# Operands of two projections split by prompt and sample columns, in a decoder layer with experts on one core

## The chip, the cores and the metric

The kernel runs on one core of a Trainium2 chip. The metric is the time of one execution on the device in microseconds (us). The engines are named as the profile does: PE (TensorE, matmul), PEld (its weight loads), DVE (VectorE), ACT (ScalarE), POOL (GpSimd) and SP (SyncE, which here only issues DMAs). A "q" behind a name (ACTq, SPq) marks what the engine's sequencer does, mostly the issue of a DMA.

## What is computed

One layer for a prompt of 512 tokens and a sample group of 8 sequences of 4 tokens (32 columns), which share all weights. Cut to what matters here:

```
z  = x @ w_in + b_in                    # split among the parts below
ya = head_norm(mlstm(...)) * sigmoid(og)        # branch A, 1024 wide
yb = sliding_window_attention(...)              # branch B, 1024 wide
mix = (sigmoid(ga) * (ya @ w_a) + sigmoid(gb) * (yb @ w_b)) @ w_out
x = LN1(ALPHA * x + mix)
x = LN2(ALPHA * x + hierarchical_moe(x))        # 32 experts
x = LN3(ALPHA * x + sigmoid(x @ w_pg) * (p @ w_pp))
```

Outputs are the new x and the new states, among them `k_s` and `v_s`: per sample sequence the last 128 rows of keys and values, of which 124 are copied from the old buffers and four are new. `p` are the embedding rows of the layer (512 + 32 rows of 256).

## The kernel before

All activations of the dense stages lie transposed: partitions are features, columns are the 544 tokens (512 of the prompt, then 32 of the samples: `NG = SEQ + NS`). A float32 operand is taken apart into a high and a low part of type fp32r (`split_from`: ACT casts the high part, L569; DVE subtracts it, L570), and a product is three matmuls (`three`, L656 to L658: high x high, high x low, low x high).

**Jobs.** A job is a block of 256 weight columns. `stream` runs the jobs in a fixed sequence: w_in's parts, among them the branch gates (GA writes `sigA`, GB writes `sigB`, four jobs each), then w_a (four jobs), w_b (four) and w_out (four). A job has two units of 128 columns. `fetch` loads the job's 1 MB of weights on SP's queue into one of two `raw` buffers, `prepare` splits a unit's weights into `wH` and `wL` (two buffers each) one unit ahead. A unit of w_a or w_b has two halves: columns 0 to 255 and 256 to 543, so that only the second half contains samples. For each of the eight 128-row blocks of the operand (k = 0 to 7) a half does three matmuls into a PSUM buffer `pj`, of which there are two. `mix_a` (L908) multiplies w_a's result with `sigA`, `mix_b` (L916, and L917 on POOL) multiplies w_b's result with `sigB`, adds, and splits the sum into `mix`, w_out's operand.

**What runs beside them.** `weave(upto, (generator, rate), ...)` runs the jobs up to a count and gives each generator so many of its steps per half unit. During GA and GB these are `swa` (the prompt's attention, with exponentials on ACT; its results go into `qsT`, which becomes `yb`) and `sample_mlstm` (it writes the sample columns of `ya` at its end). During w_a it is `sample_swa`, the samples' attention, which writes the sample columns of `qsT` (= `yb`) at its end (L1550). During w_b it is `embeddings`, which transposes the embedding rows and stores them.

**What sets the order.** The calls above give each instruction a priority. Before the kernel is built, a scheduler replays the instructions with estimated times and puts each engine's into one fixed list: an instruction goes as soon as its inputs, its buffer and its engine are free in that replay, so one of low priority can move far ahead of where it is written. On the chip each engine follows its list in order, and whatever waits there holds all that is behind it. `tc.issue_after(x)` puts DMAs behind x on their engine. A tile that takes over memory of an earlier one waits for the last user of that tile, DMAs that read it included. Pools open and close like stacks, from a left and a right end of the memory.

**The transitions that the change touches.** After GB, the sigmoids of `sigA` and `sigB` are one ACT instruction each (L1417). `split_tiles` splits `ya` into eight pieces of 544 columns (`yaH`, `yaL`). Once `ya` is split, its memory becomes `r_p`, and ACT's queue loads 2 MB of x into it (L1433). In `sample_swa`, `k_new` (the new keys, transposed back by PE and copied by ACT, L1466) and `v_new` are stored into the outputs by 16 DMAs on ACT's queue (L1557), and two DMAs on POOL copy the 124 old rows (L1555). The samples' keys come in four loads (`kb`, POOL, L1458), are transposed by PE (L1478) and copied by ACT into `KT` (L1479); L1492 are the scores, L1539 and L1546 the transposes and products of the values. After w_a, `split_tiles` splits `yb` (`ybH`, `ybL`), and the first step of `embeddings` loads the rows (`pin`, five DMAs on ACT's queue, L1575); PE transposes them (L1581), ACT copies them into `pT_in` (L1582), and a DMA stores that for later.

After w_out come the first LayerNorm and the routing, then the experts, whose weights (6 MB each) stream in through SP's queue, the first of them already during w_out, and then the tail.

Of the kernel before, what the change touches and what calls it, by code (L numbers as in the profile page):

```python
# [9 lines left out]
F32 = mybir.dt.float32  # L10
F32R = mybir.dt.float32r
# [3 lines left out]
AF = mybir.ActivationFunctionType  # L15
# [4 lines left out]
P = 128  # L20
D = 1024
KD = D // P
SEQ = 512
NT = SEQ // P
SB, ST = 8, 4
NS = SB * ST
# [4 lines left out]
WIN = 128  # L31
# [5 lines left out]
DPLE = 256  # L37
# [487 lines left out]
def tile_decoder_step(ctx: ExitStack, tc: tile.TileContext, *aps):  # L525
    nc = tc.nc
    A = dict(zip(_INS + _CONSTS + _OUT_NAMES, aps))
    sy, act, dve, pe, gp = nc.sync, nc.scalar, nc.vector, nc.tensor, nc.gpsimd

    def pool(name, bufs=1, side="left", space=None, stack=ctx):  # L530
        if space is None:
            return stack.enter_context(tc.tile_pool(name=name, bufs=bufs, side=side, reuse_waits="tile"))
        return stack.enter_context(tc.tile_pool(name=name, bufs=bufs, space=space))
# [16 lines left out]
    left = ctx.enter_context(ExitStack())  # L550
# [6 lines left out]
    right = ctx.enter_context(ExitStack())  # L557
# [7 lines left out]
    def pst(shape, tag):  # L565
        return ps.tile(shape, F32, name=tag, tag=tag)

    def split_from(H, L, src, eng=dve):
        act.copy(out=H, in_=src)  # L569
        return eng.tensor_tensor(out=L, in0=src, in1=H.bitcast(F32), op=ALU.subtract)  # L570
# [7 lines left out]
    NG = SEQ + NS  # L578
# [42 lines left out]
    for pp in range(2):  # L621
        gp.dma_start(
            out=brow[16 + 4 * pp:20 + 4 * pp, :].rearrange("j (a d) -> j a d", a=2),
            in_=b_in[C_QS + 512 * pp:C_QS + 512 * (pp + 1)].rearrange("(a j d) -> j a d", a=2, j=4),
# [136 lines left out]
    def weave(upto, *others):  # L761

        nonlocal flow
        others = [[g, rate, 0.0, True] for g, rate in others]
        while state["done"] < upto:
            next(flow)
            for o in others:
                o[2] += o[1]
                while o[3] and o[2] >= 1.0:
                    o[2] -= 1.0  # L770
                    o[3] = next(o[0], "end") != "end"
        if state["pending"]:
            state["pending"]()
            state["pending"] = None
        live = [o for o in others if o[3]]
        while live:
            live = [o for o in live if next(o[0], "end") != "end"]
# [26 lines left out]
    ya = ZA.tile([P, KD, NG], F32, name="ya", tag="za")  # L804
# [30 lines left out]
    tiles = {}  # L835
# [66 lines left out]
    N_GA, N_GB, N_WA, N_WB, N_WO = 22, 26, 30, 34, 38  # L902
# [77 lines left out]
    for r in two:  # L980
# [9 lines left out]
                   in_=wg_in[:].rearrange("p k (a b) -> p k a b", a=2))  # L990
# [84 lines left out]
    def chain(*gens):  # L1075
        for g in gens:
            yield from g
# [335 lines left out]

    weave(N_GB, (swa(), 2.6), (sample_mlstm(pool("smp", stack=sws)), 0.8))
    early.close()
    for g in (tiles["sigA"], tiles["sigB"]):
        act.activation(out=g, in_=g, func=AF.Sigmoid)  # L1417
    yb = qsT


    Z2 = pool("split", bufs=2, side="right", stack=right)

    def split_tiles(where, src, name):
        H, L = (where.tile([P, KD, NG], F32R, name=name + x, tag="split") for x in "HL")
        for k in range(KD):
            split_from(H[:, k], L[:, k], src[:, k])
        return H, L

    tiles["ya"] = split_tiles(Z2, ya, "ya")
    r_more = ZA.tile([P, NT * D + 256], F32, name="r_p", tag="za")  # L1430
    tiles["r_p"] = r_more[:, 0:NT * D].rearrange("p (t d) -> p t d", t=NT)
    shift1 = r_more[:, NT * D:]
# [2 lines left out]
    def sample_swa(Q):  # L1435
# [28 lines left out]
        for pp in range(2):  # L1464
# [4 lines left out]
                        in_=kss[:].rearrange("p a (b t) -> p a b t", t=ST))  # L1469
        yield  # L1470
        for b0 in range(0, SB, 2):
# [4 lines left out]
            for b in range(2):  # L1476
                for pp in range(2):
                    pe.transpose(out=pt[:, b, pp], in_=kb[:, b, pp * P:(pp + 1) * P], identity=ident)  # L1478
            act.copy(out=KT[:, b0:b0 + 2, :, 0:WIN].rearrange("p b a w -> p (b a) w"),  # L1479
                     in_=pt[:].rearrange("p b a w -> p (b a) w"))  # L1480
# [44 lines left out]
        def place(g):  # L1525

            pp, par = g // 2, g % 2
            return slice(64 * par, 64 * par + 64), pp, slice(64 * par + 32 * pp, 64 * par + 32 * pp + 32)

        for g in range(SKV):  # L1530
            hp, pp, rows = place(g)
            pe.matmul(pO[pp][hp], v_new[0:NS, g * SD:(g + 1) * SD], pT4[:, :, rows], start=True, stop=False)
        for b0 in range(0, SB, 2):
# [9 lines left out]
            for b in range(2):  # L1543
                for g in range(SKV):
                    hp, pp, rows = place(g)
# [3 lines left out]
        for pp in range(2):  # L1549
            dve.tensor_copy(out=qsT[:, 4 * pp:4 * pp + 4, SEQ:].rearrange("p j (b t) -> p j b t", t=ST),  # L1550
                            in_=pO[pp][:, :, 0:16].rearrange("p b (j t) -> p j b t", t=ST)[:, :, :, ::-1])
        yield
        for o, src, new in ((ko, bk, k_new[:].rearrange("s a d -> s (a d)")), (vo, bv_, v_new)):
            with tc.issue_after(last.ins):
                gp.dma_start(out=o[:, 0:WIN - ST, :], in_=src[:, ST:WIN, :])  # L1555
            for b in range(SB):
                act.dma_start(out=o[b, WIN - ST:, :], in_=new[ST * b:ST * (b + 1)])  # L1557

    with ExitStack() as scope:
        weave(N_WA, (sample_swa(pool("smp", stack=scope)), 1.5))  # L1560
    late = right.enter_context(ExitStack())
    Z3 = pool("splitb", bufs=2, side="right", stack=late)
    tiles["yb"] = split_tiles(Z3, yb, "yb")
    tiles["mix"] = tuple(Z2.tile([P, KD, NG], F32R, name="mix" + x, tag="split") for x in "HL")

    pTd = dram.tile([P, 2, NG], F32, name="pTd")

    def embeddings(Q):
        pT = Q.tile([P, 2, NG], F32, name="pT_in", bufs=1)
        pins = []  # L1570
        for t in range(NT + 1):
            rows = P if t < NT else NS
            pins.append(Q.tile([P, DPLE], F32, name="pin", bufs=NT + 1)[:rows])
            src = A["p_prompt"][0, 0, t * P:(t + 1) * P] if t < NT else A["p_sample"][0].rearrange("b t d -> (b t) d")
            act.dma_start(out=pins[t], in_=src)  # L1575
        yield
        for t, pin in enumerate(pins):
            rows = pin.shape[0]
            tp = pst([P, 2, rows], "tp")
            for k in range(2):  # L1580
                pe.transpose(out=tp[:, k], in_=pin[:, k * P:(k + 1) * P], identity=ident[:rows, :rows])  # L1581
            act.copy(out=pT[:, :, t * P:t * P + rows], in_=tp)  # L1582
            yield
        act.dma_start(out=pTd[:], in_=pT)
        yield

    with ExitStack() as scope:
        weave(N_WB, (embeddings(pool("ples", stack=scope)), 0.5))
# [145 lines left out]
    for t, st in zip(order, stats):  # L1734
        x1 = x1s[t]
        rows = x1.shape[0]
# [35 lines left out]
    with ExitStack() as scope:  # L1772
# [28 lines left out]
        def rt(name, shape, dt=F32):  # L1801
            return R.tile(shape, dt, name=name)
# [144 lines left out]
        with tc.issue_after(tokens.ins):  # L1947
# [13 lines left out]
            which = rt("which", [P, 4])  # L1961
# [44 lines left out]
    late = [(0, [(x1s[t], x1d[t * P:(t + 1) * P], "rb") for t in range(NT)] + [(*pg_half(0), "al")])]  # L2006
# [181 lines left out]
    for k in range(KD):  # L2188
        H, L, src = pg(k, 0, 512, D), pg(k, 1, 512, D), pg_in[1][:, k]
# [51 lines left out]
```

## Time and profile before

| what | value |
|---|---|
| median of 3 runs | 1151.51 us (1149.5 to 1151.61) |
| the profiled execution, its own time | 1153.13 us |
| its span, first to last instruction | 1151.3 us |
| mean granted clock of PE | 0.966 |
| PE busy | 1046.8 us (91%) |
| DVE, ACT, POOL busy | 483.7, 334.8, 245.4 us |
| HBM traffic | 248.44 MB read, 20.13 MB written |

The dense stages with w_a, w_b and w_out lie from about 457 to 640 us of the span, the experts from about 680 to 1062, the tail behind them. In a row of a timeline stand the start, the duration, the engine, the line, the operation, the tiles written and read, the shapes and how many instructions were merged; in brackets how long the engine had been idle and what ended that. In a table by stretches, each engine's busy time is followed by its count of instructions; PEclk is the clock granted to PE, where 1.00 is the full one.

### The profile page before, as it was taken

Reading aid. Unit: us, or ns where it says so; the run is one execution under the profiler, and the core shown is the slowest. Engines: PE = TensorE matmul, PEld = TensorE weight load, DVE = VectorE, ACT = ScalarE, POOL = GpSimd, SP = SyncE. Lnnn points to the kernel's source line nnn. Section 1 sums busy time; section 2 is a strip of 40 time slices with the busy share of each in tenths; the row PEclk is TensorE's granted clock in tenths of the full one; section 3 lists DMA queues with packets and bytes.
Section 4 is the critical chain, followed back from the end, with each engine's and each line's share of the span. In section 5 each row is a group of like instructions: output and inputs, shape, how many; then the busy total and the mean of one; then the engine's idle time right before and its main releaser. Section 6 shows DMA issues by size and latency. Waiting matters only on the chain. (4 is left out here: it accounts for less than half of the span.)

```text
span 1151.3 us, 26865 instructions
## 1 busy us (share of the span) xinstructions
PE 1046.8 (91%) x10359; PEld 821.0 (71%) x10360; DVE 483.7 (42%) x1245; ACT 334.8 (29%) x682; POOL 245.4 (21%) x368
## 2 busy tenths in 40 slices
PE   7999999999999999998999788775999979877987
PEld 6988999999877779898989544432555545544765
DVE  3646533546555556264566611111112111111886
ACT  5411224223454744323311311110111111212531
POOL 5000000401346562202410111101222222221021
PEclk8999999999999999898999989989899999999998
DMA  7321322223214334543389959999999999999711
GB/s 245 75 74 38 111 73 75 79 74 109 99 38 147 108 102 136 204 125 103 113 294 374 362 196 405 422 418 422 419 420 419 418 423 418 423 418 385 285 50 60
DMA packets 99024, 263.65 MB, mean 229 GB/s; under 512 B 11326, under 2 KB 58708, under 8 KB 85092
## 3 DMA queue, kind: packets, MB, share of 16 engines
q1 hardware_dynamic: 84100, 232.96, 53.0%
q0 software_dynamic: 9440, 25.24, 6.2%
q10 hardware_dynamic: 5408, 4.39, 1.3%
q8 instruction: 53, 0.87, 0.3%
q14 instruction: 23, 0.19, 0.1%
HBM read 248.44 MB, written 20.13 MB: 233 GB/s over the span
## 5 line engine op out<-in xcount | busy, mean ns | idle before, releaser
L656 PE MATMUL pj<-xH,wH 128*128 128x256 f32 (+1 forms) x672 | 197.9, 295 | 0.0
L658 PE MATMUL pj<-xH,wL 128*128 128x256 f32 (+1 forms) x672 | 197.2, 293 | 0.0
L657 PE MATMUL pj<-xL,wH 128*128 128x256 f32 (+1 forms) x672 | 196.8, 293 | 0.0
L569 ACT CAST wH<-raw 128x1024 fp32r<-128x1024 f32 x76 | 79.6, 1048 | 244.0 <-PE pj L657 155.5
L656 PEld LDWEIGHTS pj<-xH,wH 128*128 128x128 f32 x672 | 126.8, 189 | 6.3 <-issue 4.9
L658 PEld LDWEIGHTS pj<-xH,wL 128*128 128x128 f32 x672 | 126.4, 188 | 4.7 <-issue 4.3
L657 PEld LDWEIGHTS pj<-xL,wH 128*128 128x128 f32 x672 | 126.8, 189 | 2.7 <-issue 2.2
L570 DVE TENSOR_TENSOR wL<-raw,wH 128x1024 fp32r<-128x1024 f32 x76 | 94.8, 1249 | 74.0 <-ACT wH L569 72.9
L300 PE MATMUL psG<-w,xT 128*32 128x256 f32 x1152 | 73.0, 395 | 22.4 <-issue 13.8
L428 ACT ACTIVATE sg<-psG 128x128 f32<-128x128 f32 x50 | 13.9, 277 | 267.2 <-PE psG L300 267.2
L463 DVE COPY hT<-psH 128x128 f32<-128x128 f32 x50 | 14.6, 292 | 150.7 <-PE psH L305 144.5
L300 PEld LDWEIGHTS psG<-w,xT 128*32 128x32 f32 x1152 | 37.5, 112 | 49.5 <-issue 30.2
L1275 POOL TENSOR_SCALAR lg<-lg,sm 128x256 f32<-128x256 f32 (+1 forms) x64 | 55.2, 876 | 28.4 <-DVE sm L1272 17.3
L458 DVE COPY xT<-xg 128x256 f32 (+1 forms) x50 | 14.8, 295 | 109.8 <-PE psG L300 109.5
L263 POOL DMA_INDIRECT ybuf<-ysb,idy x50 | 49.5, 990 | 45.7 <-POOL idy L260 34.2
L300 PE MATMUL psG<-gu3a,xT 128*32 128x256 f32 x576 | 36.5, 395 | 14.8 <-DMA gu3a<-in_w_eu_dram 8.7
L415 ACT ACTIVATE xg<-psX,gcol 128x128 f32 (+1 forms) x100 | 36.3, 467 | 42.8 <-PE psX L293 42.8
L470 DVE SCALAR_TENSOR_TENSOR ysb<-psY,ywt,r_p 128x256 f32<-128x256 f32 x50 | 24.2, 484 | 57.1 <-PE psY L314 57.1
L656 PE MATMUL pj<-wH,xH 128*128 128x256 f32 x160 | 47.4, 296 | 0.0
L657 PE MATMUL pj<-wL,xH 128*128 128x256 f32 x160 | 45.1, 282 | 0.0
L658 PE MATMUL pj<-wH,xL 128*128 128x256 f32 x160 | 44.9, 280 | 0.0
L300 PE MATMUL psG<-w2a,xT 128*32 128x256 f32 x448 | 28.5, 397 | 14.9 <-issue 7.8
(609 smaller groups left out, 2263.3 us busy)
## 6 DMA issues: line engine op xcount, KB each, us to landing
w<-in_w_eg_dram SPq DMA_DIRECT2D x26, 1024.0 KB
w<-in_w_eu_dram SPq DMA_DIRECT2D x26, 1024.0 KB
w<-in_w_ed_dram SPq DMA_DIRECT2D x26, 1024.0 KB
raw<-in_w_in_dram SPq DMA_DIRECT2D x22, 1024.0 KB
w2d<-in_w_ed_dram SPq DMA_DIRECT2D x14, 1024.0 KB
r_p<-in_w_ed_dram SPq DMA_DIRECT2D x14, 1024.0 KB
w2a<-in_w_eg_dram SPq DMA_DIRECT2D x7, 1024.0 KB
w2a<-in_w_eu_dram SPq DMA_DIRECT2D x7, 1024.0 KB
```

The costliest lines, as they stand in the source:

```text
L263: gp.indirect_dma_start(out=ybuf.rearrange("t (q d) -> (t q) d", q=4), out_offset=bass.IndirectOffsetOnAxis(ap=idy[:, r:r + 1], axis=0), i ...
L300: m = pe.matmul(psG[32 * q:32 * q + 32], xT[:, k], W[s][half][:, :, kh, P * q:P * q + P], start=k == 0, stop=k == KD - 1)
L415: m = act.activation(out=out, in_=psX[:, k], func=AF.Identity, bias=gcol[:, 1, k:k + 1], scale=gcol[:, 0, k:k + 1])
L458: dve.tensor_copy(out=xT[:], in_=src).then_inc(S["cx"], 1)
L463: dve.tensor_copy(out=hT[:], in_=psH[:]).then_inc(S["ch"], 1)
L470: dve.scalar_tensor_tensor(out=ysb[:, r], in0=psY[:], scalar=ywt[:, bass.ds(i1, 1)], in1=shift, op0=ALU.mult, op1=ALU.add).then_inc(S["cy" ...
L569: act.copy(out=H, in_=src)
L570: return eng.tensor_tensor(out=L, in0=src, in1=H.bitcast(F32), op=ALU.subtract)
L656: pe.matmul(out, lh(k), rh(k), start=start and i == 0, stop=False)
L657: pe.matmul(out, lh(k), rl(k), start=False, stop=False)
L658: pe.matmul(out, ll(k), rh(k), start=False, stop=stop and i == len(ks) - 1)
L1275: gp.tensor_scalar(out=lg[:, par, j, 0:nk], in0=lg[:, par, j, 0:nk], scalar1=sm[:, 2, par, j:j + 1], scalar2=None, op0=ALU.mult)
```

## The change

- The sigmoids of `sigA` and `sigB` become four instructions each, for two of the eight blocks at a time. Those of `sigA` stay ahead of w_a in the program's order, those of `sigB` are woven into w_a.
- `split_tiles` splits the prompt's 512 columns only, in eight pieces, and is a generator; `split_samples` splits the 32 sample columns of all eight blocks with one cast and one subtraction. For `ya` both follow each other ahead of w_a. For `yb` the prompt's pieces are woven into w_a, and the sample pair follows behind w_a.
- The pool of the split `yb` opens ahead of w_a, under the samples' attention, on the other end of the memory.
- The embedding rows get a pool of their own that opens ahead of w_a, and are loaded by five DMAs on SP's queue, woven into w_a ahead of the pieces of `yb`. `pT_in` stays in the pool that opens at w_b, which now begins where the samples' attention had its pool.
- The new keys and values are stored by eight DMAs on POOL's queue (one per token of the four, for all eight sequences) in place of 16 on ACT's, and they stand in the `issue_after` block of the copies of the old rows.

```diff
-    for g in (tiles["sigA"], tiles["sigB"]):
-        act.activation(out=g, in_=g, func=AF.Sigmoid)
+    def sigmoids(g):
+        for i in range(0, KD, 2):
+            act.activation(out=g[:, i:i + 2], in_=g[:, i:i + 2], func=AF.Sigmoid)
+            yield
+    for _ in sigmoids(tiles["sigA"]):
+        pass
...
-    def split_tiles(where, src, name):
-        H, L = (where.tile([P, KD, NG], F32R, name=name + x, tag="split") for x in "HL")
+    def split_tiles(which, where, src, name):
+        H, L = tiles[which] = tuple(where.tile([P, KD, NG], F32R, name=name + x, tag="split") for x in "HL")
         for k in range(KD):
-            split_from(H[:, k], L[:, k], src[:, k])
-        return H, L
-    tiles["ya"] = split_tiles(Z2, ya, "ya")
+            split_from(H[:, k, 0:SEQ], L[:, k, 0:SEQ], src[:, k, 0:SEQ])
+            yield
+    def split_samples(which, src):
+        H, L = (t[:, :, SEQ:] for t in tiles[which])
+        split_from(H, L, src[:, :, SEQ:])
+    for _ in split_tiles("ya", Z2, ya, "ya"):
+        pass
+    split_samples("ya", ya)
...
             with tc.issue_after(last.ins):
                 gp.dma_start(out=o[:, 0:WIN - ST, :], in_=src[:, ST:WIN, :])
-            for b in range(SB):
-                act.dma_start(out=o[b, WIN - ST:, :], in_=new[ST * b:ST * (b + 1)])
-    with ExitStack() as scope:
-        weave(N_WA, (sample_swa(pool("smp", stack=scope)), 1.5))
+                for t in range(ST):
+                    gp.dma_start(out=o[:, WIN - ST + t, :], in_=new[t:NS:ST])
     late = right.enter_context(ExitStack())
     Z3 = pool("splitb", bufs=2, side="right", stack=late)
-    tiles["yb"] = split_tiles(Z3, yb, "yb")
+    rows_p = left.enter_context(ExitStack())
+    pin_pool = pool("pins", stack=rows_p)
+    pins = []
+    def load_rows():
+        yield
+        for t in range(NT + 1):
...
+            sy.dma_start(out=pins[t], in_=src)
+            yield
+    with ExitStack() as scope:
+        weave(N_WA, (sample_swa(pool("smp", stack=scope)), 1.5), (sigmoids(tiles["sigB"]), 1.0),
+              (chain(load_rows(), split_tiles("yb", Z3, yb, "yb")), 0.9))
+    split_samples("yb", yb)
...
     def embeddings(Q):
         pT = Q.tile([P, 2, NG], F32, name="pT_in", bufs=1)
-        pins = []
-        for t in range(NT + 1):
...
-            act.dma_start(out=pins[t], in_=src)
-        yield
```

More of the change, by code (lines that the diff above doesn't have):

```diff
@@ L1555, in sample_swa @@
                 gp.dma_start(out=o[:, 0:WIN - ST, :], in_=src[:, ST:WIN, :])
-            for b in range(SB):
-                act.dma_start(out=o[b, WIN - ST:, :], in_=new[ST * b:ST * (b + 1)])
-    with ExitStack() as scope:
-        weave(N_WA, (sample_swa(pool("smp", stack=scope)), 1.5))
+                for t in range(ST):
+                    gp.dma_start(out=o[:, WIN - ST + t, :], in_=new[t:NS:ST])
     late = right.enter_context(ExitStack())
     Z3 = pool("splitb", bufs=2, side="right", stack=late)
-    tiles["yb"] = split_tiles(Z3, yb, "yb")
+    rows_p = left.enter_context(ExitStack())
[4 more added lines that the diff above has]
+        for t in range(NT + 1):
+            rows = P if t < NT else NS
+            pins.append(pin_pool.tile([P, DPLE], F32, name="pin", bufs=NT + 1)[:rows])
+            src = A["p_prompt"][0, 0, t * P:(t + 1) * P] if t < NT else A["p_sample"][0].rearrange("b t d -> (b t) d")
+            sy.dma_start(out=pins[t], in_=src)
[4 more added lines that the diff above has]
+    split_samples("yb", yb)
     tiles["mix"] = tuple(Z2.tile([P, KD, NG], F32R, name="mix" + x, tag="split") for x in "HL")
@@ L1569, in embeddings @@
         pT = Q.tile([P, 2, NG], F32, name="pT_in", bufs=1)
-        pins = []
-        for t in range(NT + 1):
[L1572 to L1575, printed above, removed]
-        yield
         for t, pin in enumerate(pins):
```

## The prediction

> **What bounds the kernel now.** I read the busy time by stretch first, to see where TensorE stands still, then the timelines of single engines around those places.
>
> ```profile
> core 0: us, PE busy (x) PEld busy (x) DVE busy (x) ACT busy (x) POOL busy (x), PEclk, DMA share, GB/s
> 285.00:457.00 172.00, 172.00 (x1243) 140.13 (x1243) 93.86 (x326) 88.58 (x247) 77.59 (x107) 1.00 0.33 109
> 457.00:474.00 17.00, 17.00 (x138) 16.91 (x136) 6.41 (x11) 8.18 (x7) 8.35 (x15) 1.00 0.74 255
> 474.00:484.00 10.00, 7.40 (x43) 5.39 (x42) 1.74 (x3) 3.33 (x6) 1.44 (x2) 0.66 0.47 164
> 521.00:535.00 14.00, 10.36 (x70) 9.74 (x67) 7.72 (x14) 6.09 (x12) 0.54 (x1) 0.76 0.51 116
> 664.00:684.00 20.00, 18.00 (x100) 10.94 (x104) 4.42 (x22) 4.25 (x8) 2.35 (x3) 0.82 0.31 113
> 709.00:1062.00 353.00, 291.56 (x4571) 162.94 (x4561) 58.85 (x187) 61.49 (x148) 68.54 (x114) 0.96 1.02 419
> ```
>
> From 285 to 474, TensorE (PE) is busy all the time: the dense stages are bound by it, and work of other engines beside it is free. In the w_a and w_b stages it has two holes, 474 to 484 and 521 to 535, each followed by a spell at a lower granted clock (0.66 and 0.76 on average). From 709 to 1062 DMA is full with expert weights. That stream is not tied to the clock on the wall: in 664 to 684 DMA is only 31% busy, because the prefetched buffers are full and the stream waits for the experts to start. So what the dense stages save moves the whole rest forward.
>
> **Hole A (in w_a).** Timelines of ACT and PE:
>
> ```profile
> 459.31 0.41 ACTq L1433 DMA_DIRECT2D r_p<-in_x_prompt_dram  x1
> 464.29 10.78 ACTq L1557 DMA_DIRECT2D out_dram<-k_new  x8
> 465.82 0.66 ACTq L1557 DMA_DIRECT2D out_dram<-k_new  x2
> 473.17 1.90 ACTq L1557 DMA_DIRECT2D out_dram<-k_new  x2
> 475.17 1.04 ACT L569 CAST wH<-raw 128x1024 fp32r<-128x1024 f32 x1 [9.96 <-DMA raw<-in_w_a_dram]
> 476.12 0.58 ACT L1479 COPY KT<-tp 128x512 f32<-128x512 f32 x1
> 470.32 0.60 PE L1478 MATMUL tp<-keep,kb 128*128 128x128 f32 x4
> 470.67 0.36 PE L656 MATMUL pj<-yaH,wH 128*128 128x256 f32 x1
> 470.87 0.29 PE L657 MATMUL pj<-yaL,wH 128*128 128x256 f32 x1
> 472.52 0.30 PE L656 MATMUL pj<-yaH,wH 128*128 128x288 f32 x1
> 473.86 0.29 PE L657 MATMUL pj<-yaL,wH 128*128 128x288 f32 x1
> 476.75 0.65 PE L1492 MATMUL nm<-KT,QT 64*32 64x132 f32 x4 [2.60 <-ACT KT L1479]
> 483.49 0.29 PE L658 MATMUL pj<-yaH,wL 128*128 128x288 f32 x1
> 484.30 0.43 PE L1492 MATMUL nm<-KT,QT 64*32 64x132 f32 x8
> 484.66 0.39 PE L658 MATMUL pj<-yaH,wL 128*128 128x256 f32 x1
> ```
>
> PE waits for the first KT copy, which stands on ACT behind the w_a cast, and that stands behind the eight DMA issues of k_new. An issue takes 0.3 to 0.4 us, yet the eight last 10.78 us: the sixth ends at 466.48, the last two come at 473.17 and just before 475. By the semaphores in the trace, the hardware DMAs of SP and ACT share eight completion semaphores in turn, and these two issues wait until the previous users of theirs have landed: the 2 MB load of r_p from 459.31 and a w_a fetch. So ACT stands still for transfers that nobody there needs.
>
> The size: at full rate a 288-wide matmul takes 0.134 us (473.86 - 472.52, ten steps), a 256-wide one 0.118 (472.52 - 470.87, 14 steps), four transposes 0.35 (470.67 - 470.32), eight score products 0.36 (484.66 - 484.30). From 474.00 to 483.62, PE did 16 score products (0.72), 8 transposes (0.70) and 13 wide matmuls (1.74): 3.2 us of work in 9.6. Hole A costs 6.4 us.
>
> **Hole B (start of w_b).**
>
> ```profile
> 520.64 0.66 PE L1546 MATMUL sp<-pT_s,kb 128*64 128x32 f32 x16
> 521.23 0.49 DVE L1550 COPY qsT<-sp 128x128 f32<-128x128 f32 x2
> 521.57 0.64 ACT L569 CAST ybH<-qsT 128x544 fp32r<-128x544 f32 x1
> 521.69 1.23 DVE L570 TENSOR_TENSOR wL<-raw,wH 128x1024 fp32r<-128x1024 f32 x1
> 521.76 1.80 ACTq L1575 DMA_DIRECT2D pin<-in_p_prompt_dram  x1
> 522.26 0.39 PE L656 MATMUL pj<-ybH,wH 128*128 128x256 f32 x1 [0.96 <-ACT ybH L569]
> 522.84 5.17 DVE L570 TENSOR_TENSOR ybL<-qsT,ybH 128x544 fp32r<-128x544 f32 x8
> 524.45 0.66 PE L1581 MATMUL tp<-keep,pin 128*128 128x128 f32 x2 [1.67 <-DMA pin<-in_p_prompt_dram]
> 527.48 0.66 PE L1581 MATMUL tp<-keep,pin 128*128 128x128 f32 x2 [1.00 <-DMA pin<-in_p_prompt_dram]
> 534.34 0.30 PE L658 MATMUL pj<-ybH,wL 128*128 128x288 f32 x1
> ```
>
> Each of the eight splits of yb covers all 544 columns, so none starts before the sample columns of qsT are written (521.72); then PE waits for splits and, in its own order, for the embedding rows. From 521.2 to 534.48 it did one unit of w_b, 24 x 0.118 + 24 x 0.134 = 6.05 us, and five transposes, 0.44: 6.5 us of work in 13.3. Hole B costs 6.8 us.
>
> **The change, part by part.**
>
> Stores of new keys and values: 16 ACT issues become 8 on GpSimd, behind the two 992 KB copies. With them goes ACT's standstill, so hole A goes: -6.4 us. What is late next there is the KT copy itself, right after its transposes (470.67 plus 0.58), before PE needs it at 474.00.
>
> ```profile
> 513.66 0.60 POOL L1555 DMA_DIRECT2D out_dram<-in_state_swa_k_dram  x1
> out_dram<-in_state_swa_k_dram POOLq DMA_DIRECT2D x1, 992.0 KB, 8.2
> out_dram<-in_state_swa_v_dram POOLq DMA_DIRECT2D x1, 992.0 KB, 9.5
> POOL sigA L917 <- DVE sigB L916: 19.6, 1, 19.6
> ```
>
> GpSimd pays 8 x 0.60 = 4.8 us, inside 19.6 us in which it waits for w_b's first result. Its own DMAs also wait in turn; the longest such wait is a 992 KB landing, 8.2 us. Behind the eight issues on its queue is only the first sum of w_b (L917), which nothing on PE needs at once. Without that cover the cost is 4.8 to 13 us of GpSimd time.
>
> yb: the prompt parts (8 casts of about 0.6, 8 subtractions of about 0.65 us) move into w_a, where they may run once the attention of the prompt is done; ACT was busy 8.18 of 17 us there, with the standstill counted as idle. They go one by one, so a waiting cast of weights loses at most 0.64 us. What is left at w_b's start is one pair for 256 sample columns: 521.72, plus at most 0.64 and 0.65, with the weight cast and its subtraction (1.0 and 1.2 us) perhaps ahead of them. Only the second half of the first unit needs it, 24 x 0.118 = 2.8 us after 521.2. Between 0 and 1.5 us is left of the hole by this; I take 0.5.
>
> Embedding rows: five issues move from ACT (one took 1.80 us) to SP, into w_a, and PE's two waits (1.67 and 1.00) go. On SP they stand among the w_a and w_b fetches; 0.5 MB more run beside r_p and a w_a fetch, at the 255 GB/s of that stretch 2.1 us. That fetch had landed by 475. Its cast comes due when the unit ends whose second half starts at 472.52 (at full rate 24 x 0.134 = 3.2 us later, 475.7), and the next unit covers six us more, of which cast and subtraction take 2.3: I take 0; if the fetch were 6 us later it would cost 2 to 3.
>
> A new wait: the transposed rows (pT_in) now lie where the sample attention's pool begins, over k_new, and their first copy on ACT must wait for the k_new stores. Those queue behind the 992 KB copy, which landed at 513.66 + 8.2 = 521.9, 0.7 us after w_b could begin, plus the four stores. The third transpose of rows waits for that copy's buffer on PE. Bounds: 0, and 6.8 (all of hole B back). I take 1.5, nearer to the lower end, as the landing is only 0.7 us late.
>
> ya: the pieces narrow from 544 to 512 columns and one sample pair comes on top, at most 0.64 + 0.65 us; PE has no hole at w_a's start (17.00 of 17.00 busy), so 0; uncovered, 1.3.
>
> Sigmoids: 3.84 us at once becomes four pieces of about 1 us each. The pieces can go where the scheduler finds ACT free, as the whole one did:
>
> ```profile
> L829 ACT ACTIVATE sigA<-pj,bcol x8: 480/494/495, 293.7 to 378.0; 128x288 f32<-128x288 f32 x8
> 380.57 1.28 ACT L1417 ACT_TABLE_LOAD   x1
> 381.87 3.84 ACT L1417 ACTIVATE sigA<-sigA 128x4352 f32<-128x4352 f32 x1
> 385.99 1.28 ACT L1269 ACT_TABLE_LOAD   x1
> ```
>
> It ran right after its last input (378.0), between exponentials, with a table load on each side: 6.7 us of ACT. Each of sigA's four pieces can have such a pair, and sigB's first two as well if they fall among the attention's exponentials: five more blocks of 1.28 + 1 + 1.28 = 3.6 us, 18 us on ACT, which was busy 88.58 of 172. The 6.7 us block left PE at 172.00 of 172.00, so I take 0. Bounds: 0 and 18.
>
> [...]
>
> **Sum.** -6.4 - 6.8 + 0.5 + 1.5 = -11.2 us. The profiled execution took 1153.13 us with a span of 1151.3, so it would take 1141.9; it lies 1.6 above the median of the runs, 1151.51, and against that the sum gives 1140.3. The runs lie within 2.1 us; 0.2% (2.3 us) is about what a measurement can tell from none.
>
> **Rivals.**
>
> Slower, by sigmoid pieces: if PE stood still for each of the five added blocks, because its accumulators are emptied and its weights cast by ACT, the sum is 1140.3 + 18 = 1158. It decides from 2.3 us lost per block (11.2 / 5). For it: the pieces can only go into the exponentials. Against: the full PE row around a longer block. [...]
>
> A wait takes hole B's place: pT_in behind k_new holds ACT, and with it the sample split and the casts. If the stores land 5 us after w_b's start instead of 1 to 2, it costs about 3.5 more plus the low clock after a hole (2 us): 1140.3 + 5.5 = 1146. For it: the second copy landed 9.5 us after its issue, and stores go in the same queue.
>
> Not what it says: hole A stays, because other DMAs in w_a (the rows on SP) wait in turn for the same r_p load and hold the fetches behind them: 1140.3 + 6.4 = 1147. Against: SP has six us in hand there.
>
> [...]
>
> Same: the expert stream swallows it, 1151. For it: 419 GB/s from 709 on. Against: DMA's lull before.
>
> **How the numbers follow.** Forecast 0.60 (1137.5 to 1143.5); the new wait 0.13 and hole A staying 0.09 (both to 1148); slower 0.10; same 0.05; the rest, 0.03, is faster than 1137. Faster than 0.2%: 0.60 + 0.13 + 0.09 + 0.03 = 0.85. The range from 1137 to 1148 holds 0.82.
>
> **What would show it.** Right: no row of ACT issuing k_new, no wait of PE for KT over 1 us, casts of ybH during w_a, clock 1.00 in both stages, w_b's first matmuls right after the last of w_a, the first expert transpose some 11 us earlier. Wrong: a PE gap at w_b's start ended by ACT pT_in; more than ten table loads with PE idle before 457; a w_a fetch that ends a wait of the cast.

## The result, and the profile after

The changed kernel takes 1145.1 us (median of 20 runs, 1142.19 to 1150.82) against 1150.33 us of the kernel before (20 runs, 1146.79 to 1157.08): a ratio of 0.995, 95% interval 0.9934 to 0.9965, so 4 to 7.6 us faster (5.8 by the ratio, 5.2 by the medians). The forecast was 1140.3, which was 11.2 us less than its own baseline. The profiled execution took 1144.28 us with a span of 1142.3.

Both holes are gone. The busy time by stretch of the changed kernel; the last three stretches answer to 521:535, 664:684 and 709:1062 of before, moved by what the dense stages won:

```profile
core 0: us, PE busy (x) PEld busy (x) DVE busy (x) ACT busy (x) POOL busy (x), PEclk, DMA share, GB/s
285.00:457.00 172.00, 172.00 (x1245) 140.14 (x1244) 94.74 (x330) 102.93 (x260) 78.56 (x109) 1.00 0.34 112
474.00:484.00 10.00, 10.00 (x106) 8.24 (x105) 4.06 (x7) 3.23 (x5) 2.16 (x3) 1.00 0.54 179
517.00:531.00 14.00, 14.00 (x114) 14.00 (x113) 6.71 (x12) 4.43 (x7) 4.17 (x7) 1.00 0.31 76
654.00:674.00 20.00, 17.99 (x108) 11.03 (x110) 4.42 (x22) 3.96 (x7) 2.36 (x3) 0.84 0.33 115
699.00:1052.00 353.00, 292.09 (x4554) 163.08 (x4550) 58.40 (x184) 61.01 (x148) 68.61 (x113) 0.95 1.02 419
```

PE is full and at full clock where it was 7.40 of 10 and 10.36 of 14 busy at 0.66 and 0.76. In w_a, ACT now has no DMA issue of k_new between its casts, and the prompt part of yb goes there (timeline of ACT), while GpSimd issues the stores behind the two copies (timeline of POOL):

```profile
460.40 0.35 ACT L1478 COPY k_new<-tp 32x256 f32<-32x256 f32 x1
460.65 1.11 ACT L1419 ACTIVATE sigB<-sigB 128x1088 f32<-128x1088 f32 x1
461.67 3.21 ACT L569 CAST ybH<-qsT 128x512 fp32r<-128x512 f32 x6
465.08 1.05 ACT L569 CAST wH<-raw 128x1024 fp32r<-128x1024 f32 x1 [0.21 <-PE pj L657]
466.60 0.59 ACT L1491 COPY KT<-tp 128x512 f32<-128x512 f32 x1 [0.46 <-PE tp L1490]
...
507.64 2.10 POOL L1569 DMA_DIRECT2D out_dram<-k_new  x4
516.63 1.03 POOL L1569 DMA_DIRECT2D out_dram<-v_new  x2 [3.42 <-DMA out_dram<-in_state_swa_k_dram]
521.36 0.73 POOL L917 TENSOR_TENSOR sigA<-sigA,sigB 128x256 f32<-128x256 f32 x1 [3.70 <-DVE sigB L916]
```

In this pair of profiles the whole forecast is there: the last product of w_b starts at 567.32 instead of 577.62 and the first expert's transpose at 669.17 instead of 679.57, 10.4 us earlier. Yet the medians differ by 5.2. The experiments ask where the other half is.

### The profile page after: what moved, and what is told of

Its sections match the earlier page's. It is cut to its first block, busy times and chain, and to the rows that moved or that the text cites. A ratio compares the mean times of both kernels' runs of the same rounds, so it can differ in the third digit from the quotient of the medians.

```text
span 1142.3 us, 26870 instructions
## 1 busy us (share of the span) xinstructions
PE 1043.9 (91%) x10359; PEld 819.3 (72%) x10360; DVE 484.3 (42%) x1247; ACT 346.7 (30%) x698; POOL 249.9 (22%) x376
```

## The experiments

All ratios are to the kernel before, run beside them, five rounds, with the 95% interval.

**Both kernels once more.** No edit.

> The kernel before, unchanged, for a second profile. The changed kernel's dense stages gained 12.3 us from the first matmuls after the start to the first expert transpose, but the medians of 20 runs moved only 5.2. Theory A (spread): the trace of before first shown was simply a slow execution; in a second one the holes in w_a and w_b are as long as in the first within 1 us, and the experts take some 3 us less than the 384.4 us (first transpose to last down product) of the first. Theory B (the holes vary): the holes are together several us shorter in this execution than 13.2.

> The changed kernel, unchanged, for a second profile. Theory A (spread): dense stages as in the first trace, no hole in w_a or w_b, first expert transpose at 667 to 669 us; five rounds give a ratio to before of 0.990 to 0.998. Theory C (the experts give it back): the experts take 4 to 5 us longer than in both traces of before, again and again, so that the sum of the parts is the 5 us measured.

Before: 1152.16 us, ratio 1.0012 (0.9991 to 1.0033). After: 1145.41 us, 0.9949 (0.9925 to 0.9972). The gain of 5 to 6 us is firm. But the second profile of the kernel before is another one than the first: the same holes, at two thirds of the price. Here is hole A in three stretches of 3.41 us of the busy time view (length, PE's busy time, and so on; the granted clock is third from the end), before (first three lines) and again_before:

```profile
473.04:476.45 3.41, 1.11 (x9) 0.87 (x7) 0.20 (x1) 1.28 (x2) 0.00 (x0) 1.00 0.24 87
476.45:479.86 3.41, 3.11 (x16) 1.79 (x16) 1.36 (x2) 0.83 (x2) 0.73 (x1) 0.50 0.31 105
479.86:483.28 3.42, 3.42 (x20) 2.88 (x20) 0.00 (x0) 0.90 (x2) 0.71 (x1) 0.50 0.98 345
...
475.24:478.66 3.42, 1.55 (x14) 0.97 (x15) 1.56 (x2) 2.04 (x3) 0.24 (x1) 1.00 0.01 2
478.66:482.07 3.41, 3.41 (x21) 2.69 (x20) 0.00 (x0) 0.98 (x3) 1.20 (x2) 0.50 0.96 323
482.07:485.48 3.41, 3.41 (x34) 3.07 (x33) 2.00 (x4) 1.05 (x1) 0.00 (x0) 1.00 0.37 143
```

In the 14 profiles the granted clock stood at 0.50 only in pieces of 3.41 us (or multiples), on a grid whose phase against the kernel's start differs from profile to profile (0.3 to 3.2 us). How busy PE was in a stretch went with the clock of the next one, as counted over the grid stretches that have a clock on record for themselves and for the next (4622):

```
at full clock, PE busy under 0.40 of the stretch:  next one at 0.50 in  117 of 118
               0.40 to 0.50:                                            21 of 57
               over 0.50:                                               40 of 4164
at 0.50,       PE busy under 0.75:                 next one at 0.50 in   73 of 73
               0.75 to 0.85:                                            33 of 44
               over 0.85:                                               13 of 166
```

So, by these counts, a gap of 2.3 us may or may not leave one stretch under 0.40 busy (2.05 us idle); it depends on where the grid falls. In again_before the grid cuts the gap: the stretch shown is 0.45 busy (1.55 of 3.42) and one of the 21 that a low one followed. Each piece costs a full PE 1.7 us, an estimate from its length and its clock (3.41 x 0.50).

**Half of the change at a time.** Stores alone, and yb's prompt part and rows alone (both with whole sigmoids):

```diff
 # stores_only: the kernel before with
-            for b in range(SB):
-                act.dma_start(out=o[b, WIN - ST:, :], in_=new[ST * b:ST * (b + 1)])
+                for t in range(ST):
+                    gp.dma_start(out=o[:, WIN - ST + t, :], in_=new[t:NS:ST])
 # yb_rows_only: the kernel before with split_tiles, split_samples and load_rows of the change
```

> Before, with the 16 stores of new keys and values on ACT replaced by eight on GpSimd, nothing else. My theory: hole A (474 to 484) is gone, the first expert transpose comes 6.4 us earlier than in before (679.6 less 6.4 = 673.2, start-up aside), the hole at w_b's start stays at about 6.8. Rival (issue time only): only the eight issues of 0.3 to 0.4 us are saved, the gain is under 3 us and PE still waits for KT.

> Before, with ya and yb split by prompt and sample columns, yb's prompt part and the embedding rows during w_a; the stores stay on ACT's queue and the sigmoids stay whole. My theory: the hole at w_b's start is gone (6.8 us), the hole in w_a stays or grows, since the five loads of rows take turns with the stores' DMAs; first expert transpose 5 to 7 us earlier than in before. Rival: the ACT standstill now also holds the pieces of yb, so that w_b still waits, gain under 3 us.

Stores alone: 1155.18 us, 1.0035 (1.0013 to 1.0057). Yb and rows alone: 1150.65 us, 1.0001 (0.9981 to 1.002). Neither gains what I expected; together with the rest they gain 5 to 6. PE's waits from 470 to 530 (total, number, longest), stores_only first, then yb_rows_only:

```profile
PE tp L1581 <- DMA pin<-in_p_prompt_dram: 2.9, 1, 2.9
PE pj L656 <- ACT ybH L569: 1.0, 1, 1.0
PE pj L657 <- DVE ybL L570: 0.8, 1, 0.8
...
PE nm L1499 <- ACT KT L1486: 2.3, 1, 2.3
```

Each closes its own hole. But with hole A closed, PE comes to w_b 4.5 to 5.4 us earlier (first product 516.8, against 522.3 in before and 521.3 in again_before). The idle time of hole B grows, from 3.6 and 2.3 us to 4.7: the rows' loads are issued when w_b begins, and PE's transposes of rows begin 7.6 us after the first of these issues, against 3.8 us in the kernel before (520.68 to 524.45). That the 992 KB copies beside them are the reason is my reading (timelines of POOL and ACT, stores_only; the second copy landed at 521.5, 10.6 us after its issue, and the transposes of rows began at 522.8):

```profile
510.90 0.61 POOL L1555 DMA_DIRECT2D out_dram<-in_state_swa_v_dram  x1
515.24 0.36 ACTq L1575 DMA_DIRECT2D pin<-in_p_prompt_dram  x1
516.33 0.34 ACTq L1575 DMA_DIRECT2D pin<-in_p_prompt_dram  x1
L1581 PE MATMUL tp<-keep,pin x4: 415/421/446, 522.8 to 524.8; 128*128 128x128 f32 x4
```

**Stores alone, again.** No new edit.

> The kernel before with the stores on GpSimd alone, once more, because the first time it came out 4 us slower than the kernel before while its dense stages were no longer. If that was a chance of its clock pieces (7 of 3.41 us between w_b and the experts, 5 in the comparison) and of the late last expert weights (PE waited 2.5 us), the time comes to 1149 to 1152 now. If it belongs to the kernel, it comes to 1154 to 1156 again, and the trace again shows PE waiting 2.5 us at the last expert, and a wait of over 4 us in all at the start of w_b.

1152.96 us, 1.0004 (0.998 to 1.0028). The wait for rows is there again, 3.4 us, so stores alone win nothing; that they lose 4 us was partly chance. That they lose something (1.0035 and 1.0004) stays open.

**Which half of hole B.** Stores with the rows early, and stores with the yb split, each without the other:

```diff
 # stores_rows: stores_only with load_rows in w_a, yb split whole after it
+        weave(N_WA, (sample_swa(pool("smp", stack=scope)), 1.5), (load_rows(), 0.9))
 # stores_yb: stores_only with yb's prompt part split in w_a, rows still on ACT in embeddings
+        weave(N_WA, (sample_swa(pool("smp", stack=scope)), 1.5),
+              (split_tiles("yb", Z3, yb, "yb"), 0.9))
```

> The kernel before with the stores on GpSimd and the embedding rows loaded on SP during w_a; yb is still split whole, behind the sample columns, and the sigmoids are whole. Two looks at stores alone showed hole A gone, and hole B with 4.7 and 5.2 us of PE standing still, of which the rows' landing made 2.9 and 3.4; those rows were issued 515 to 518 and landed behind the 992 KB copies. Theory 'rows took it': with the rows early that part goes; 1.0 us (ybH) and at most 1.5 us (splits) of standing still remain, at a low clock in some executions only: 1147 to 1150. Rival 'both parts are needed': PE, no longer held by rows, waits for the splits instead, which come one in 0.65 us, eight in 5.2: 1150 to 1153.

> The kernel before with the stores on GpSimd and yb's prompt part split during w_a; the rows are still loaded on ACT when w_b begins, and the sigmoids are whole. Theory 'rows took it': the waits for ybH and ybL go, and the wait for the rows remains if their products stand as early in PE's order as before (2.9 to 3.4 us and the clock behind it: 1149 to 1153); if the schedule puts them later, because nothing of w_b waits any more, there is no wait and the time is that of the changed kernel, 1145 to 1147. Rival: the splits are hole B's whole price and the rows none: 1145 to 1147 with a wait for rows still in the trace.

Stores and rows: 1146.5 us, 0.9963 (0.9945 to 0.998), PE without a gap over 0.5 us from 470 to 530: the change's gain without the yb split. Stores and yb: 1148.01 us, 0.998 (0.9961 to 1.0), one gap of 1.06 us in w_a (for a weight split on DVE) and none in w_b, because PE's order now has the rows' products later (the first at 526.6). With A closed, hole B is closed with either half, but in both runs the order changed with the edit. In stores_rows PE also does the last value products of the samples at 512.95 instead of 515.21, so that the casts of yb begin at 513.9 instead of 516.1, while PE still has products of w_a to do. What each half is worth at an unchanged order is not shown.

**The change without its stores, and without its pieces.** The two remaining parts taken back, one each:

```diff
 # act_stores_back: the changed kernel with
-                for t in range(ST):
-                    gp.dma_start(out=o[:, WIN - ST + t, :], in_=new[t:NS:ST])
+            for b in range(SB):
+                act.dma_start(out=o[b, WIN - ST:, :], in_=new[ST * b:ST * (b + 1)])
 # whole_sigmoids: the changed kernel with
+    for g in (tiles["sigA"], tiles["sigB"]):
+        act.activation(out=g, in_=g, func=AF.Sigmoid)
```

> The changed kernel with the sixteen stores of new keys and values put back on ACT. Six profiled executions so far show the granted clock at 0.50 only in pieces that are multiples of 3.41 us, and a piece follows a stretch in which PE stood still. Theory 'clock by chance': hole A comes back with 2.3 to 2.6 us of PE standing still (the wait for KT), plus no, one or two pieces of low clock at 1.7 us of lost work each, other in each execution; so the time goes from 1145.4 to between 1147.5 and 1151, and the rest of the stage stays as in the changed kernel (no wait for embedding rows, no wait for ybH). Rival 'full price': the hole costs the 6.4 us that I summed from one profile in every execution: 1151.8. Rival 'stores gain nothing': stores on GpSimd alone made the kernel before 4 us slower, so taking them off again makes the changed kernel faster or leaves it: 1145.5 or less.

> The changed kernel with the two sigmoids whole, both ahead of w_a, as in the kernel before. Theory 'clock by chance': the eight pieces cost nothing, since PE is busy 172.00 of 172.00 us from 285 to 457 with them too; the time stays at 1145.4 within 2.5, with four or five table loads of ACT instead of thirteen. Rival 'given back': the missing 5 us of the forecast are the pieces' table loads, which delay casts; without them the time falls to 1140 to 1142.

Whole sigmoids: 1146.41 us, 0.9954 (0.993 to 0.9978). The pieces cost nothing, nor do they win. Stores back on ACT: 1145.53 us, 0.9952 (0.9928 to 0.9976): hole A does not come back, against all I expected. ACT stands still all the same, up to the issue at 472.78 (ACT's timeline). The load of r_p was issued at 459.99. That the issue waits for its landing is my estimate from the trace of before, where the eight issues of k_new take eight semaphores in turn, the seventh that of the r_p load, and it came at 473.17, 0.02 us after the last landing on it (473.15):

```profile
463.12 0.26 ACTq L1569 DMA_DIRECT2D out_dram<-k_new  x1
472.78 0.61 ACTq L1569 DMA_DIRECT2D out_dram<-k_new  x2
473.44 0.59 ACT L1491 COPY KT<-tp 128x512 f32<-128x512 f32 x1 [8.40 <-PE tp L1490]
```

But it ends at 472.78, and the transposes that this KT copies begin at 472.6 (470.32 in the kernel before); PE loses nothing. In the kernel before a table load and a sigmoid of 3.85 us stand on ACT ahead of k_new's issues; here a piece of 1.11 us does, and the w_a cast comes after the KT copy, not ahead of it. In yb_rows_only, which differs from this kernel by the whole sigmoids alone, the last of these issues end at 476.64, the cast comes ahead of the KT copy, and PE stands still for 2.3 us. So in these schedules either part, stores on GpSimd or sigB in pieces, closes hole A (the pieces by this one profile).

**A hole of the same kind elsewhere, closed, and filled.** In the routing stage PE waits 5.05 us for ACT's copy of plo, which stands in ACT's order behind a copy of At (L1986) that waits for DVE:

```diff
 # plo_first: the changed kernel, before_plo_first: the kernel before, each with
         for t, out in zip((0, KD), A32):
-            act.copy(out=out, in_=At[:, t:t + out.shape[1]])
+            with tc.issue_after(copied[7].ins):      # the copy of plo for n = 7
+                act.copy(out=out, in_=At[:, t:t + out.shape[1]])
 # warm_router: the changed kernel with five products nobody reads, in the wait
+        for _ in range(5):
+            with tc.issue_after(behind_pm.ins):
+                behind_pm = pe.matmul(junk, ident, keep[:, 0:256], start=True, stop=True)
```

> The changed kernel with one edit outside the change: in the routing stage the two ACT copies of At wait in ACT's order behind the two copies of plo, not ahead of them. In the changed kernel's trace PE waits 5.05 us there for ACT's copy of plo, which stands behind a copy of At that waits 7.8 us for VectorE; it is a hole of the same kind as hole A, and 6.83 us of low clock follow it. Theory 'clock by chance': with the hole the low clock behind it goes as well, and all that follows moves forward by it: 5.0 us of standing still less what At then bounds (PE's next product needs At, ready some 2 us before it), plus 1.7 to 3.4 us of clock: 1145.4 to between 1137 and 1141. Rival 'swallowed': the expert stream takes up what is won ahead of it, since its prefetch is bounded by DMA: 1144 to 1146. Rival 'idle only': the low clock has another cause than the hole and stays: 1141 to 1142.

> The changed kernel with five products on TensorE that nobody reads (128x128 by 128x256, about 0.79 us each by the like ones at the tail) in the routing stage, where PE waits 5.05 us for plo. They fill some 4 us of the wait and do not shorten it. Theory 'clock by chance': the low clock there follows from PE standing still, so with the wait filled the 6.83 us (twice) at 0.50 that came behind it are gone, and the stage from w_b's last unit to the first expert falls from 46.5 to 48.2 us to 43 to 45.5; time 1141.5 to 1144. Rival 'other cause': the clock falls because of the stage's narrow products or by itself: pieces of low clock remain at the same place, stage 46 to 48, time 1145.5. Rival 'in the way': the products are late and hold the next ones back: 1146 to 1147.

> The kernel before, with plo's copies ahead of At's on ACT in the routing stage and nothing else. In the changed kernel that edit took the stage from 46.5 to 48.2 us to 39.5 and the time from 1145.4 to 1138.3. If the two gains are of different places and add up, the kernel before goes from 1152 to 1144.5 to 1146, which leaves the change worth 6 to 7 us beside it. If both drew on the same slack, that of the expert stream, the edit gains less here, 1148 or more.

plo_first: 1138.33 us, 0.9884 (0.9847 to 0.9921), the fastest of all. before_plo_first: 1144.09 us, 0.9943 (0.9924 to 0.9962). The two gains add up: 0.9884 / 0.9943 = 0.9941, so beside this edit the change is worth 6.8 us (some 2 to 12 by the two intervals). warm_router: 1146.81 us, 0.9957 (0.9935 to 0.9979). PE's timelines of after, plo_first and warm_router:

```profile
651.54 1.93 PE L1811 MATMUL pj<-gu3b 128*32 128x256 f32 x16 [5.05 <-ACT plo L1816]
653.41 3.77 PE L1808 MATMUL kept<-gu3b 128*128 128x512 f32 x4
...
645.22 1.07 PE L1813 MATMUL pj<-gu3b 128*32 128x256 f32 x16
646.22 1.98 PE L1810 MATMUL kept<-gu3b 128*128 128x512 f32 x4
...
645.37 2.43 PE L1929 MATMUL sp<-keep 128*128 128x256 f32 x10
650.49 1.07 PE L1811 MATMUL pj<-gu3b 128*32 128x256 f32 x16 [2.69 <-ACT plo L1816]
651.49 1.98 PE L1808 MATMUL kept<-gu3b 128*128 128x512 f32 x4
```

After the wait the same products take 1.93 and 3.77 us, without the wait 1.07 and 1.98. And with the wait half filled by work for nobody they take 1.07 and 1.98 too. The five products took 2.43 us, not the 4 that I expected, and 2.69 us of the wait were left. Here the grid cuts this rest (two stretches, 0.51 and 0.70 busy); whole in one stretch, it would have left less than 0.40. So the filled run alone proves little, but all profiles together do: in each of the 11 with the wait of 5.05 us whole, a spell of two or three pieces of low clock begins during the wait, and in plo_first, before_plo_first and warm_router none begins there. By these profiles the low clock at this place came from PE standing still. The stage from the last but one product of w_out to the first expert took 46.51 and 48.22 us in the two profiles of the changed kernel, 44.69 when filled, 39.53 when closed. Filling gave the total nothing: another piece (10.24 us from 659.7) followed the narrow products behind it, and PE waited 3.0 us at the last expert in that execution. Whether that wait belongs to the kernel is open.

## Why the prediction was right or wrong

All profiles together, from the first product of w_a to the last of w_b (108.33 us without a gap, in five profiles to the hundredth). "Idle" is PE's gaps over 0.5 us, "pieces" the stretches of 3.41 us at 0.50:

```
                  idle A  idle B  pieces   stage over 108.33   idle + 1.7 x pieces
before             2.60    3.63     4            12.1                13.0
again_before       2.33    2.32     2             8.0                 8.1
before_plo_first   1.43    2.04     0             3.8                 3.5
stores_only        0       4.68     3             8.5                 9.8
stores_again       0       5.22     2             7.3                 8.6
yb_rows_only       2.30    0        1             4.5                 4.0
stores_yb          1.06    0        0             1.1                 1.1
act_stores_back, whole_sigmoids, stores_rows
                   0       0        0          0.0 to 0.6             0
after, again_after, warm_router, plo_first
                   0       0        0             0.0                 0
```

The first three have the same code in these stages. The waits of the third, and its clock, in the same stretches as before:

```profile
PE nm L1492 <- ACT KT L1479: 1.4, 1, 1.4
PE tp L1581 <- DMA pin<-in_p_prompt_dram: 1.1, 1, 1.1
PE pj L656 <- ACT ybH L569: 1.0, 1, 1.0
474.00:484.00 10.00, 8.57 (x79) 7.05 (x77) 3.39 (x6) 4.07 (x6) 1.45 (x2) 1.00 0.57 191
515.00:570.00 55.00, 52.96 (x427) 52.15 (x428) 30.19 (x50) 20.16 (x36) 19.14 (x22) 1.00 0.41 126
```

By its own steps:

- **The step that failed is the size of the holes**, "Hole A costs 6.4 us" and "Hole B costs 6.8 us". Both are nearly right for the execution that I read (12.1 of the 13.2 are in the stage), and wrong as the price in a typical one: of the 13.2, 6.2 was idle time and the rest low clock, and the low clock is a matter of where the grid falls. Three profiles of the same code give 12.1, 8.0 and 3.8 us, 8.0 in the mean; their idle time alone is 6.2, 4.7 and 3.5. The gain of 4.0 to 7.6 us lies within what three so different samples allow, so no place has to be found where time was given back. In single profiles none shows: from the first expert to the end the two profiles of before took 471.8 and 472.5 us, those of after 473.2 and 473.6, the others 470.9 to 476.0 without order. The table leaves two things open. By it yb_rows_only should be 3.5 us faster than the three profiles of before in the mean, and stores_yb 6.9; the runs give 0 (2.3 slower to 2.2 faster) and 2.3 (0 to 4.5). If the holes typically cost the 5.8 that the change gained, 1.3 and 4.7 would be left to expect; whether the rest is chance, one profile of each cannot tell.
- **The baseline** was good (1151.51; 127 runs of the kernel before have a median of 1151.55). I set the sum against the profiled execution, 1.6 us above the median, and took that off the end result, but not off the holes, where it may have come from.
- **"With them goes ACT's standstill, so hole A goes"**: hole A went, and alone the stores close it too, but only move the loss to w_b; without them it stays closed (act_stores_back). In the finished change the runs show no worth of the stores' place (ratios to before 0.9952 without and 0.9949 with them, each within 0.0024, so a worth of 6.4 us is out). ACT's standstill was real, 9.66 us between the issues at 463.12 and 472.78, and still cost nothing (PE 9.92 of 10.00 us busy from 474 to 484, at full clock).
- **yb and rows**: hole B went. I counted both halves as needed; with A closed each alone does it, in the order that came with it.
- **The sample split left over, 0.5, and the new wait, 1.5**: both were 0. The first product of w_b starts 0.13 us after the last of w_a, and PE's only wait from 285 to 580 is this one:

```profile
PE pj L656 <- DVE r_p L940: 0.3, 1, 0.3
```

- **The sigmoid pieces at 0**: right. ACT does 102.93 us in 285 to 457 instead of 88.58 (14.4 more, where I had bounded 18), has 11 table loads there instead of two, and PE stays at 172.00 of 172.00. The rival of 1158 fell. What I missed is that the pieces also clear ACT's queue ahead of hole A.
- **Rows on SP, stores on GpSimd, ya: 0**, right; no wait of PE came of them.
- **"What the dense stages save moves the whole rest forward"**: right; the rival "same" fell. The edit plo_first, just ahead of the experts, reaches the end of both kernels, by 7 us.
- **The time** fell in the range, but in the part that I had kept for two rivals, the new wait (1146) and hole A staying (1147), and neither took place. The 2 us of low clock after a hole in the first of these sums were my estimate; the profiles showed none to four pieces of 1.7 us for the two holes together. The range held for another reason than the one given, which is luck.

## What to carry to other kernels

A hole on TensorE had two prices here: its idle time, and pieces of low clock behind it that came by chance of the execution. Both varied: the same two holes had 6.2, 4.7 and 3.5 us of idle time and 4, 2 and 0 pieces. Read the two apart, and from several profiles, before you add them to a forecast. Here two waits followed each other, and closing the first alone only let the second be met earlier and wait longer (hole B 4.68 and 5.22 us idle, against 3.63, 2.32 and 2.04): before you credit a part with a hole, ask what else closes it, and what the next hole becomes. And look in every engine's order for a copy that waits, ahead of one that somebody else waits for: moving it gained some 7 us here, about as much as the whole change.

## What the hardware showed

- The granted clock, as counted above over 14 profiles: pieces on a grid of 3.41 us, whose phase differed (0.3 to 3.2 us); behind a stretch under 0.40 busy the next was at 0.50 in 117 of 118; a low spell ended behind 153 of 166 stretches over 0.85 busy, against 11 of 44 at 0.75 to 0.85. In again_before a gap of 2.33 us brought a piece.
- The busy share alone did not tell it: the stretches over 0.50 that were still followed by low clock held, for the most part (29 of 40), narrow products (36 or 40 columns, or 48 rows) over more than 0.3 of their length. Another 82 such stretches were not followed by low clock, and why is open.
- A store issued on GpSimd took 0.52 to 0.55 us to issue, and the later ones waited 3.42 us in its queue for the landing of a 992 KB copy (the changed kernel's profile).
